# A row-wise log-softmax whose tiles take every second row of 64 instead of 32 neighbouring rows

## The chip, the core and the metric

The kernel runs on one core of a Trainium2 chip. The core has five engines with their own instruction queues: TensorE (PE) for matrix products, VectorE (DVE) for elementwise work and reductions, ScalarE (ACT) for functions such as the exponential, GpSimd (POOL) and SyncE (SP), which here only issues loads. Data move between the chip's main memory (DRAM, also called HBM) and the on-chip memory (SBUF, 128 partitions) by 16 DMA engines, which serve the transfers that SP and ACT issue. Engines are kept in step by semaphores. The metric is the time of one execution on the device in microseconds (us); less is better.

## The reference

The input is 16 x 512 x 50000 numbers of type float32, that is 8192 rows of 50000. Each row is treated by itself:

```python
max_x = np.max(x, axis=-1, keepdims=True)
shifted = x - max_x
log_sum_exp = np.log(np.sum(np.exp(shifted), axis=-1, keepdims=True))
return (shifted - log_sum_exp).astype(np.float32)
```

The input has 1638.4 MB, and so has the output. Each element is read once and written once.

## The kernel before

The 8192 rows are cut into 256 tiles of 32 rows. A row of 50000 is cut into G = 4 runs of 12500, and each run lies in a partition of its own, so that a tile fills 128 partitions x 12500 elements (6.4 MB). The partition number is 4 times the row's number in the tile plus the number of the run. Four buffers (`NBUF`) of that size take turns: tile t lies in buffer t mod 4, is worked on in place and is stored from there.

For a whole tile, VectorE takes the maximum over four columns of 3125 elements (line 221), ScalarE the exponential of each with its sum (line 276), VectorE joins the maxima of the four partitions of a row through a transposition of 32 x 32 blocks (lines 188 to 204), TensorE adds the four partial sums of a row with a matrix of ones (line 330), ScalarE takes the logarithm (line 264), and VectorE subtracts both from the tile (line 209). Since a row's four runs are always four neighbouring partitions, these steps do not depend on which rows of the input a tile holds.

Tile 0 is treated another way, so that work can start early. It is cut by rows into `NS` = 4 parts of 8 rows. A row is then cut into 16 runs of 3125, so that a part fills 128 partitions x 3125 elements. Each part has a load of its own (line 163) and a store of its own (line 268). The last tile is stored in four pieces by columns.

Order is written out by hand. SP issues the four part loads, then the loads of tiles 1 to 3, and then, for each further tile, waits until the buffer that it needs has been stored (`take(sync, stored[j])`) and issues the load (line 160). Tiles 5 and on are issued in a loop on the device, where a tile's place in DRAM is worked out from the loop's counter; the helper `run` makes the access pattern for that from the list of all tiles. ScalarE issues the store of a tile after the second of the four exponentials of the next tile (`GATE` = 2), for tiles 1 and on in a loop of the same kind. A transfer counts its semaphore up by 16 when it is complete.

In DRAM a tile of before is one piece: its 32 rows are neighbours, so its 128 runs of 12500 elements follow each other, and the access pattern has 128 runs at a step of 12500. A part of tile 0 has 128 runs of 3125 at a step of 3125. On the SBUF side there are 128 partitions in both.

Of the kernel before, what the change touches and what calls it, by code (L numbers as in the profile page):

```python
# [16 lines left out]
G = 4  # L17
R = P // G
C = 3125
NBUF = 4  # L20

NS = 4

GATE = 2
GS = G * NS
RS = P // GS
# [20 lines left out]
def take(engine, sem, n=16):  # L47

    engine.wait_ge(sem, n).then_inc(sem, -n)  # L49


def cols(c):
    return slice(c * C, (c + 1) * C)
# [3 lines left out]
def kernel(  # L57
# [6 lines left out]
    xf = x.flatten_outer_dims()  # L64
    of = out.flatten_outer_dims()
# [3 lines left out]
    ntiles = N // R  # L69


    rounds = (ntiles - NBUF) // NBUF
    assert ntiles % NBUF == 0 and rounds >= 2
    tail = range(1 + rounds * NBUF, ntiles)

    xt = xf.rearrange("(t r) (g w) -> t (r g) w", r=R, g=G)
    ot = of.rearrange("(t r) (g w) -> t (r g) w", r=R, g=G)
    xs = xf.rearrange("(t s r) (g w) -> t s (r g) w", s=NS, r=RS, g=GS)
    os = of.rearrange("(t s r) (g w) -> t s (r g) w", s=NS, r=RS, g=GS)

    def run(a, first, n):

        part = a[first : first + NBUF * n].rearrange("(q i) p w -> q i p w", i=NBUF)
        return lambda q, i: part[bass.ds(q, 1), i].rearrange("o p w -> (o p) w")

    data = ctx.enter_context(tc.tile_pool(name="data", bufs=1))
    stats = ctx.enter_context(tc.tile_pool(name="stats", bufs=1))
# [10 lines left out]
    bufs = [data.tile([P, W], FP32, name=f"buf{j}") for j in range(NBUF)]  # L98
# [41 lines left out]
    @block.gpsimd  # L140
    def _(gpsimd):
        k = 0
        for g in (GS, G):
            view = ones[g].rearrange("p (r g) -> p r g", g=g)
            r = P // g
            gpsimd.memset(ones[g], 1.0).then_inc(ready)
            gpsimd.affine_select(  # L147
                out=view, in_=view, pattern=[[-g, r], [0, g]], base=0,
                channel_multiplier=1, compare_op=ALU.is_ge, fill=0.0,
            ).wait_op(ready, k + 1, "sem-ge").then_inc(ready)  # L150
            gpsimd.affine_select(  # L151
                out=view, in_=view, pattern=[[g, r], [0, g]], base=g - 1,
                channel_multiplier=-1, compare_op=ALU.is_ge, fill=0.0,
            ).wait_op(ready, k + 2, "sem-ge").then_inc(ready)
            k += 3

    @block.sync
    def _(sync):
        def load(j, src):
            sync.dma_start(out=bufs[j], in_=src).then_inc(landed[j], 16)  # L160

        for s in range(NS):
            sync.dma_start(out=bufs[0][:, cols(s)], in_=xs[0, s]).then_inc(
                landed_part[s], 16
            )
        for t in range(1, NBUF):
            load(t, xt[t])
        take(sync, stored[0], 16 * NS)
        load(0, xt[NBUF])
        src = run(xt, NBUF + 1, rounds - 1)  # L170
        with sync.Fori(0, rounds - 1) as q:
            for i in range(NBUF):
                j = (i + 1) % NBUF
                take(sync, stored[j])
                load(j, src(q, i))
        for t in tail:
            take(sync, stored[t % NBUF])
            load(t % NBUF, xt[t])
        for j in range(NBUF - 1):
            take(sync, stored[j])  # L180
        take(sync, stored[NBUF - 1], 16 * NS)
# [78 lines left out]
    @block.scalar  # L260
    def _(scalar):
        def log(k):
            added.next(
                scalar.activation(out=logs[k], in_=rowsums[k], func=ACT.Ln)  # L264
            ).then_inc(logged.sem)

        def store(j, dst, buf):
            subtracted.next(scalar.dma_start(out=dst, in_=buf)).then_inc(stored[j], 16)

        def whole(j, dst=None):  # L270

            for c in range(NS):
                if c == GATE and dst is not None:
                    store((j - 1) % NBUF, dst, bufs[(j - 1) % NBUF])
                shifted.next(
                    scalar.activation(  # L276
                        out=dump, in_=bufs[j][:, cols(c)], func=ACT.Exp,
                        bias=negms[j][:, c : c + 1], scale=1.0,
                        accum_out=parts[j][:, c : c + 1],
                    )  # L280
                ).then_inc(on_act.sem)
                on_act.next(scalar.nop())  # L282
            agreed.next(
                scalar.activation(  # L284
                    out=scales[j], in_=negms[j], func=ACT.Exp,
                    bias=negmaxs[j][:, 0:1], scale=-1.0,
                )
            ).then_inc(rescaled.sem)
            log(j)

        def in_parts(j, t):
            for s in range(NS):
                agreed.next(
                    scalar.activation(  # L294
                        out=dump, in_=bufs[j][:, cols(s)], func=ACT.Exp,
                        bias=negmaxs[NBUF + s][:, 0:1], scale=1.0,
                        accum_out=sub_sum[:, s : s + 1],
                    )
                ).then_inc(summed_part.sem)
                if s:  # L300
                    store(j, os[t, s - 1], bufs[j][:, cols(s - 1)])
                log(NBUF + s)
            store(j, os[t, NS - 1], bufs[j][:, cols(NS - 1)])

        def settle():
            for count in (on_act, shifted, agreed, added, subtracted):
                count.settle(scalar)

        nc.scalar.preload_act_table_set("natural_log_exp_and_others")  # L309
        in_parts(0, 0)  # L310
        settle()
        whole(1)
        settle()
        dst = run(ot, 1, rounds)
        with scalar.Fori(0, rounds) as q:
            for i in range(NBUF):
                whole((i + 2) % NBUF, dst(q, i))
            settle()
        for t in tail[1:-1]:
            whole(t % NBUF, ot[t - 1])  # L320
        store(t % NBUF, ot[t], bufs[t % NBUF])
        whole(NBUF - 1)
        for c in range(NS):
            store(NBUF - 1, ot[ntiles - 1][:, cols(c)], bufs[NBUF - 1][:, cols(c)])

    @block.tensor
    def _(tensor):
# [58 lines left out]
```

## Time and profile before

| | |
|---|---|
| median of 5 runs | 7586.57 us (7585.56 to 7593.28) |
| the profiled execution: its time, and its span on the page | 7587.51 us, 7585.8 us |
| VectorE busy | 5444.0 us (72%) |
| ScalarE busy | 3184.9 us (42%) |
| TensorE busy | 478.2 us (6%) |
| bytes moved by DMA, mean rate | 3276.85 MB, 432 GB/s |
| load of a tile (255), from issue to landing | 36.7 us (median) |
| store of a tile (254), from issue to landing | 41.7 us (median) |
| load of a part of tile 0 (4) | 11.4 us (median; 6.5 to 16.3) |
| store of a part of tile 0 or a piece of the last tile (8) | 18.9 us (median) |

The span runs from the first to the last instruction; the execution's own time also has what lies around it, here 1.7 us. A busy share is an average over the span. A row of slices shows the span in 40 equal pieces, each with a digit for tenths of busy time. In a row of waits stand the instruction that waited, what released it, and then the time in total, how often, and the longest. DVEq and SPq are the queues of VectorE and SP; line 49 is the helper `take`, which waits for a transfer's semaphore. A DMA queue's row has its packets, its megabytes and its share of the time of 16 engines; q1 holds the loads and q10 the stores. A transfer is made of packets, here one for each run, and of small ones that count up the semaphore.

### The profile page before, as it was taken

The page shows a single profiled execution, that of the slowest core. Times are in us where ns is not written, and L with a number is a line of the kernel's source. Part 1 is how long each engine was busy: PE and PEld are TensorE (multiplying, and loading weights), DVE is VectorE, ACT ScalarE, POOL GpSimd, SP SyncE. Part 2 cuts the span into 40 slices and gives each one's busy share as a digit, 9 for nine tenths or more (in the row PEclk, how much of TensorE's full clock was granted, in tenths as well). Part 3 has the DMA queues.
Part 4 walks back from the last instruction along what each step waited for, and adds up shares of the span by engine and source line. Part 5 has one row for each costly group of instructions (what it writes and reads, how often), then busy time and mean ns, then how long its engine had stood idle before and what let it go on. Part 6 is the DMA issues. An engine that isn't in the chain of part 4 may idle for free. (4 is left out here: it accounts for less than half of the span.)

```text
span 7585.8 us, 13839 instructions
## 1 busy us (share of the span) xinstructions
PE 478.2 (6%) x2048; PEld 456.0 (6%) x2048; DVE 5444.0 (72%) x2832; ACT 3184.9 (42%) x2563; POOL 2.3 (0%) x10
## 2 busy tenths in 40 slices
PE   0000000000000000000000000000000000000000
PEld 0000000000000000000000000000000000000000
DVE  7777777777777777777777777777777777777776
ACT  4344443444434444344443444434444343444433
POOL 0000000000000000000000000000000000000000
DMA  9999999999999999999999999999999999999999
GB/s 423 433 433 434 433 433 433 435 434 433 435 432 434 433 433 434 433 432 435 431 434 434 431 434 433 432 433 432 435 433 432 434 432 433 433 432 434 431 434 398
DMA packets 75026, 3276.85 MB, mean 432 GB/s; under 512 B 8336, under 2 KB 8336, under 8 KB 8336
## 3 DMA queue, kind: packets, MB, share of 16 engines
q1 hardware_dynamic: 37296, 1638.42, 50.0%
q10 hardware_dynamic: 37728, 1638.42, 50.0%
q14 instruction: 2, 0.02, 0.0%
HBM read 1638.40 MB, written 1638.40 MB: 432 GB/s over the span
## 5 line engine op out<-in xcount | busy, mean ns | idle before, releaser
L276 ACT ACTIVATE dump<-buf,negm 128x3125 f32<-128x3125 f32 x1020 | 2925.7, 2868 | 3787.1 <-DVE negm L221 3748.8
L221 DVE TENSOR_REDUCE negm<-buf 128x1 f32<-128x3125 f32 x1020 | 3405.0, 3401 | 912.1 <-DVEq L49 912.1
L209 DVE TENSOR_SCALAR buf<-buf,negmax,logsum 128x12500 f32<-128x12500 f32 (+1 forms) x262 | 1739.6, 6641 | 553.5 <-ACT logsum L264 553.5
L330 PE MATMUL sums<-scaled,ones 128*128 128x1 f32 x2040 | 475.9, 355 | 7054.4 <-DVE scaled L232 7054.4
L330 PEld LDWEIGHTS sums<-scaled,ones 128*128 128x128 f32 x2040 | 454.0, 327 | 7076.3 <-DVE scaled L232 7076.3
L232 DVE TENSOR_TENSOR scaled<-scale,part 128x4 f32<-128x4 f32 x255 | 41.5, 163 | 577.7 <-ACT scale L284 577.7
L264 ACT ACTIVATE logsum<-sums 128x1 f32<-128x1 f32 x259 | 44.3, 171 | 551.5 <-PE sums L330 548.8
L276 ACT ACTIVATION_READ_ACCUMULATOR dump<-buf,negm 128x1 f32 x1020 | 190.0, 186 | 0.0
L284 ACT ACTIVATE scale<-negm,negmax 128x4 f32<-128x4 f32 x255 | 75.8, 297 | 23.5
L226 DVE TENSOR_REDUCE negp<-negm 128x1 f32<-128x4 f32 x255 | 40.1, 157 | 39.0 <-DVE negm L221 39.0
L204 DVE STREAM_TRANSPOSE negmax<-spread 128x32 f32<-128x32 f32 x259 | 54.9, 212 | 9.0
L188 DVE STREAM_TRANSPOSE allneg<-negp 128x32 f32<-128x32 f32 x259 | 54.8, 212 | 9.0
L191 DVE TENSOR_REDUCE rowneg<-allneg 128x8 f32<-128x32 f32 (+1 forms) x259 | 48.2, 186 | 9.0
L198 DVE COPY spread<-rowneg 128x32 f32<-128x32 f32 x259 | 47.0, 181 | 9.0
L239 DVE TENSOR_REDUCE negp<-buf 128x1 f32<-128x3125 f32 x4 | 13.6, 3400 | 7.6 <-DVEq L49 7.6
L294 ACT ACTIVATE dump<-buf,negmax 128x3125 f32<-128x3125 f32 x4 | 11.5, 2869 | 14.5 <-DVE negmax L204 14.5
L341 PE MATMUL sums<-sub_sum,ones 128*128 128x1 f32 x8 | 2.3, 363 | 29.6 <-ACT dump L294 29.6
L341 PEld LDWEIGHTS sums<-sub_sum,ones 128*128 128x128 f32 x8 | 2.0, 312 | 29.9 <-ACT dump L294 29.9
L309 ACT ACT_TABLE_LOAD x1 | 1.3, 1283 | 1.0 <-SPq L118 1.0
L147 POOL TENSOR_SCALAR_AFFINE_SELECT ones<-ones 128x128 f32<-128x128 f32 x2 | 0.9, 442 | 0.1
L151 POOL TENSOR_SCALAR_AFFINE_SELECT ones<-ones 128x128 f32<-128x128 f32 x2 | 0.9, 429 | 0.1
L294 ACT ACTIVATION_READ_ACCUMULATOR dump<-buf,negmax 128x1 f32 x4 | 0.7, 186 | 0.0
(5 smaller groups left out, 0.8 us busy)
## 6 DMA issues: line engine op xcount, KB each, us to landing
buf<-in_x_dram SPq DMA_DIRECT2D x255, 6250.0 KB, 36.7
out_dram<-buf ACTq DMA_DIRECT2D x254, 6250.0 KB, 41.7
out_dram<-buf ACTq DMA_DIRECT2D x8, 1562.5 KB, 18.9
buf<-in_x_dram SPq DMA_DIRECT2D x4, 1562.5 KB, 11.4
```

Of the source, the lines that this page charges most:

```text
L188: vector.transpose(out=allneg, in_=negp.to_broadcast([P, SQ]))
L191: vector.tensor_reduce(out=rowneg[:, : SQ // g], in_=allneg.rearrange("p (r g) -> p r g", g=g), op=op, axis=AX, negate=negate,)
L198: vector.tensor_copy(out=spread.rearrange("p (r g) -> p r g", g=g), in_=rowneg[:, : SQ // g, None].to_broadcast([P, SQ // g, g]),)
L204: vector.transpose(out=negmaxs[k], in_=spread)
L209: ins = vector.tensor_scalar(out=buf, in0=buf, scalar1=negmaxs[k][:, 0:1], scalar2=logs[k], op0=ALU.add, op1=ALU.subtract,)
L221: vector.tensor_reduce(out=negms[j][:, c : c + 1], in_=bufs[j][:, cols(c)], op=ALU.max, axis=AX, negate=True,).then_inc(shifted.sem if c < ...
L226: vector.tensor_reduce(out=negp, in_=negms[j], op=ALU.min, axis=AX).then_inc(on_dve.sem)
L232: vector.tensor_mul(out=scaleds[j], in0=scales[j], in1=parts[j])
L264: scalar.activation(out=logs[k], in_=rowsums[k], func=ACT.Ln)
L276: scalar.activation(out=dump, in_=bufs[j][:, cols(c)], func=ACT.Exp, bias=negms[j][:, c : c + 1], scale=1.0, accum_out=parts[j][:, c : c + 1],
L284: scalar.activation(out=scales[j], in_=negms[j], func=ACT.Exp, bias=negmaxs[j][:, 0:1], scale=-1.0,)
L330: ins = tensor.matmul(rowsums[j], ones[G], scaleds[j][:, c : c + 1], start=c == 0, stop=c == NS - 1,)
```

## The change

A tile now takes 32 rows out of 64 neighbouring ones, every second row. Tiles 0 and 1 share the first 64 rows: tile 0 has the even ones, tile 1 the odd ones; tiles 2 and 3 share the next 64, and so on. The parts of tile 0 take 8 of 16 neighbouring rows in the same way. Loads and stores use the same rows, so the output is the same.

In DRAM a tile becomes 32 rows at a step of 100000 elements (400000 bytes), each with 4 runs of 12500; the access pattern has three dimensions, 32 x 4 x 12500. A part of tile 0 becomes 8 rows at that step, each with 16 runs of 3125: 8 x 16 x 3125. The SBUF side still has 128 partitions, and which partition holds which row and run of the tile is as before. The number and size of the runs, the order of all instructions and all semaphores are as before.

The helper `combs` makes the list of tiles and the array with the half (`h`) as its first dimension; `run` now picks the half and the pair of tiles from the tile's number, and steps by k = 2 pairs from one pass of the loop to the next.

```diff
-    xt = xf.rearrange("(t r) (g w) -> t (r g) w", r=R, g=G)
-    ot = of.rearrange("(t r) (g w) -> t (r g) w", r=R, g=G)
-    xs = xf.rearrange("(t s r) (g w) -> t s (r g) w", s=NS, r=RS, g=GS)
-    os = of.rearrange("(t s r) (g w) -> t s (r g) w", s=NS, r=RS, g=GS)
-
-    def run(a, first, n):
-
-        part = a[first : first + NBUF * n].rearrange("(q i) p w -> q i p w", i=NBUF)
-        return lambda q, i: part[bass.ds(q, 1), i].rearrange("o p w -> (o p) w")
+
+    def combs(a):
+        both = a.rearrange("(t r h) (g w) -> h t r g w", h=2, r=R, g=G)
+        return [both[t % 2, t // 2] for t in range(ntiles)], both
+
+    (xt, xh), (ot, oh) = combs(xf), combs(of)
+    xs, os = (
+        a.rearrange("(t s r h) (g w) -> h t s r g w", h=2, s=NS, r=RS, g=GS)[0]
+        for a in (xf, of)
+    )
+
+    def run(both, first, n):
+
+        k = NBUF // 2
+
+        def tile_of(q, i):
+            h, t = (first + i) % 2, (first + i) // 2
+            part = both[h, t : t + k * (n - 1) + 1 : k]
+            return part[bass.ds(q, 1)].rearrange("o r g w -> (o r) g w")
+
+        return tile_of
...
-        src = run(xt, NBUF + 1, rounds - 1)
+        src = run(xh, NBUF + 1, rounds - 1)
...
-        dst = run(ot, 1, rounds)
+        dst = run(oh, 1, rounds)
...
-            store(NBUF - 1, ot[ntiles - 1][:, cols(c)], bufs[NBUF - 1][:, cols(c)])
+            store(NBUF - 1, ot[ntiles - 1][:, :, cols(c)], bufs[NBUF - 1][:, cols(c)])
```

## The prediction

> **What bounds the kernel now.** I read the page's slices first, then the DMA part, then the busiest groups, then the waits.
>
> ```profile
> span 7585.8 us, 13839 instructions
> ...
> DVE  7777777777777777777777777777777777777776
> ACT  4344443444434444344443444434444343444433
> ...
> DMA  9999999999999999999999999999999999999999
> ...
> DMA packets 75026, 3276.85 MB, mean 432 GB/s; under 512 B 8336, under 2 KB 8336, under 8 KB 8336
> ...
> q1 hardware_dynamic: 37296, 1638.42, 50.0%
> q10 hardware_dynamic: 37728, 1638.42, 50.0%
> ...
> HBM read 1638.40 MB, written 1638.40 MB: 432 GB/s over the span
> ```
>
> The DMA engines are full in all 40 slices and the two queues take half of their time each.[...] So time is bytes over the rate of 16 DMA engines: 432 / 16 = 27.0 GB/s each. One number is for later: the 8336 smallest packets are 16 x (259 loads + 262 stores). These are the completion marks: today every transfer runs on all 16 engines and leaves one mark per engine.
>
> The waits of VectorE and of the load queue say the same:
>
> ```profile
> DVE negm L221 <- DVEq L49: 912.1, 252, 4.8
> ```
>
> ```profile
> SPq L49 <- SPq L49: 7429.7, 256, 74.1
> ```
>
> VectorE idles 912.1 / 252 = 3.6 us per tile until its tile has landed, and the load queue waits 7429.7 / 256 = 29.0 us per tile for a buffer to be stored. Both wait for the DMA engines. The stretches (columns: length, busy time of PE, PEld, DVE, ACT, POOL, clock, DMA share, GB/s) show where the engines are not full:
>
> ```profile
> 0.00:75.00 75.00, 4.22 (x16) 3.79 (x16) 56.29 (x39) 33.34 (x28) 2.30 (x10) 1.00 0.97 411
> 75.00:150.00 75.00, 5.60 (x24) 5.34 (x24) 58.02 (x32) 32.66 (x27) 0.00 (x0) 1.00 1.01 429
> 3000.00:3100.00 100.00, 7.46 (x32) 7.12 (x32) 68.79 (x41) 41.12 (x36) 0.00 (x0) 1.00 1.01 435
> 7530.00:7586.00 56.00, 3.73 (x16) 3.56 (x16) 28.78 (x16) 13.10 (x14) 0.00 (x0) 1.00 0.74 315
> ```
>
> The start is full after the first 2.5 us. Only the last 56 us, with the last tile's arithmetic between its load and its store, have room. Work added to a DMA engine at the start therefore moves the end.
>
> The trace's packet records, which no printed view lists, add two things. A packet of 50,000 bytes takes 1.847 us and one of 12,500 bytes 0.467 us, nearly all of them to within 1%: an engine serves them one by one at 27 GB/s, whatever the address. And the completion marks of one engine come later and later: 2.6 us behind the first at load 8, 4.0 at load 60, 16.6 from load 120 to the last. The other fifteen need 29.52 us per tile (loads 20 to 60); 198 more tiles at that rate put their last load 20.6 us before the laggard's. So one lagging engine sets the end, and its number isn't recorded.
>
> **The change, part by part.** Arithmetic, its order, semaphores and buffers are untouched: every engine has the same instructions in the same order. All 521 transfers get another DRAM pattern; each still moves one run of 50,000 or 12,500 bytes per partition, so bytes and data packets stay.
>
> *Whole tiles (255 loads, 254 stores, and the last tile's four stores by columns).* The DRAM side goes from 128 runs in a row to 32 rows of 4 runs, one row in two left out. [...] Packets stay at 1.847 us: cost 0. [...] Our row pitch becomes 400,000 bytes, no power of two, and the flat 1.847 us says that the engine limits, not the memory. [...]
>
> *Issue.* A DMA issue takes 0.33 us on SP (L160). If a third dimension doubled it, 255 issues cost SP 84 us, inside its 7429.7 us of waiting, and ScalarE's queue 262 x 0.34 = 89 us, inside its 3748.8 us of waiting for L221. Behind such a store on ScalarE stand two exponentials, for which VectorE would wait. A load's start would be 0.33 us later, which is covered while other transfers are queued: 36.7 us to land a load and 41.7 for a store make 78.4 us in flight per tile of 29.6, 2.6 transfers at any time. Without that cover: +84. I take 0.
>
> *Tile 0 (four loads, L163, and four stores).* Here the DRAM side becomes 8 rows of 16 runs, in place of 128 runs. [...] Each of engines 0 to 7 then gets 64 loads and 64 stores of 12,500 bytes instead of 32 and 32, and engines 8 to 15 none. At today's 0.467 us that is 64 more packets x 0.467 = +29.9 us on engines that have no free time until the tail.
>
> *Which partitions these 8 engines reach.* With 128 partitions on 8 engines, the plain share is 16 neighbours each. [...] Each part then takes two shares: 0.934 us instead of 0.467. Tile 0 costs an engine 128 x 0.934 = 119.6 us against 64 x 0.467 = 29.9: +89.7. [...] Three share a port then, for some 55 us (3 tiles x 8 packets x 1.847 = 44.3, slowed by about a fifth): 55 / 1.40 = 39 packets instead of 59, 20 x 0.934 = +18.5. Sum on the slowest engines: +108. If sharing hurts loads only, or stores only, half of the 90 goes: 45 + 18.5 = +63.
>
> [...]
>
> *What is late next.* The first part lands at about 25 us (2.5 + 16 packets x 1.40) instead of 7.6, the fourth near 100 (its packets alternate with the first stores by then), tile 0 is stored some 108 us later than today, and so the load that waits for buffer 0 (the first wait on SP, 74.1 us today) starts that much later. VectorE needs 25.9 us per tile from the start of one maximum to the next (37.79 to 63.68 us), less than 29.6, so it adds nothing; nor can it catch up, since the DMA engines set the pace.
>
> *The laggard.* If it is one of 0 to 7, all of +108 reaches the end. If it is one of 8 to 15, engines 0 to 7 must first use up the 20.6 us that they are ahead: +87. I take the middle, +98. Sum against the profiled execution: 7587.5 + 98 = 7685. Its 7587.5 lies 0.9 above the median, nothing beside these costs.
>
> **Rivals.**
>
> *No port sharing.* Eight engines, each packet at 0.467 us: +30 with the laggard below 8, 7617. For it: the trace has never shown a slow port. [...]
>
> *Not slower: the laggard hides it.* Again no port sharing, and the lagging engine among 8 to 15. Engines 0 to 7 are then +29.9 - 20.6 = +9 against today's end: 7597, within 0.2%. It decides as long as tile 0's extra stays below 20.6 + 15 = 36 us; with shared ports it can't.
>
> *The split doesn't change.* The parts still run on 16 engines: 7587. [...]
>
> [...]
>
> *The lag goes.* Another address pattern frees the laggard: 20.6 us less, 7567, and nothing added.
>
> **How the numbers follow.** Shared ports 0.60, with its own range from +63 - 20.6 = +42 (7630) to +108 (7696). No sharing 0.20, half of it (laggard below 8) at 7617 and half at 7597. Split unchanged 0.07. Whole tiles slower 0.10. Lag gone 0.03. A measurement tells apart about 0.2%, 15 us. Slower: 0.60 + 0.10 + 0.10 = 0.80; same: 0.10 + 0.07 = 0.17; faster 0.03. The range reaches from 7595, below the +9 case, to 7706, leaving out the unchanged split, the freed lag and the slow tiles.
>
> **What will show it.** Smallest packets 8336 - 8 x 8 = 8272 say that eight transfers ran on 8 engines; 8336 say the split stayed. The L163 loads landing after about 25 to 100 us say shared ports; 9 to 40 say twice the packets at full speed; 6.5 to 16.3 no change. The DMA share in the first 100 us must fall, since engines 8 to 15 run dry. In the middle, 435 GB/s per stretch says that whole tiles are untouched. The prediction is wrong if the middle slows, or if paired engines fall out of step so that ports cost little.

## The result and the profile after

The changed kernel takes 7666.17 us (median of 29 executions, 7656.88 to 7699.93); the kernel before, on the same chips, 7588.06 us (median of 52). The difference of the medians is 78.1 us. The ratio of the mean times is 1.0082, 95% interval [1.0063, 1.0101]: slower by about 1%. (Some executions of most kernels here, of the one before too, take mostly 80 to 150 us longer: 10 of the 52 before took 7666 to 7683 us and pull this ratio down, which is 1.0105 without them, and the longest are left out of the ratios below.) The profiled execution took 7664.22 us with a span of 7662.5 us, 76.7 us more than before.

The rates of the 40 slices before:

```profile
GB/s 423 433 433 434 433 433 433 435 434 433 435 432 434 433 433 434 433 432 435 431 434 434 431 434 433 432 433 432 435 433 432 434 432 433 433 432 434 431 434 398
```

The slices and the DMA part of the page of the changed kernel:

```profile
span 7662.5 us, 13839 instructions
...
DVE  4677777777777777777777777777777777777776
...
DMA  8999999999999999999999999999999999999999
GB/s 243 431 433 434 432 434 434 434 432 433 434 433 432 434 432 434 432 434 432 434 433 432 434 434 433 432 434 434 431 434 434 434 432 434 433 431 434 434 434 403
DMA packets 74962, 3276.85 MB, mean 428 GB/s; under 512 B 8272, under 2 KB 8272, under 8 KB 8272
...
q1 hardware_dynamic: 37264, 1638.42, 50.1%
q10 hardware_dynamic: 37696, 1638.42, 49.6%
```

Two readings matter. The loss is in the first slice, which moved 243 GB/s where it had moved 423; from the second slice on the rate is that of before. And the small packets are 8272 = 8336 - 8 x 8: eight transfers now leave eight marks instead of sixteen, four of them loads (q1 has 32 packets fewer) and four stores (q10 likewise). These are tile 0's.

When tile 0's parts land is seen where VectorE begins their maxima (timelines: start, duration, engine, line, what). Before:

```profile
7.63 3.41 DVE L239 TENSOR_REDUCE negp<-buf 128x1 f32<-128x3125 f32 x1 [7.63 <-DVEq L49]
11.89 3.40 DVE L239 TENSOR_REDUCE negp<-buf 128x1 f32<-128x3125 f32 x1
17.92 3.40 DVE L239 TENSOR_REDUCE negp<-buf 128x1 f32<-128x3125 f32 x1
23.96 3.40 DVE L239 TENSOR_REDUCE negp<-buf 128x1 f32<-128x3125 f32 x1
```

In the changed kernel:

```profile
23.80 3.41 DVE L251 TENSOR_REDUCE negp<-buf 128x1 f32<-128x3125 f32 x1 [23.80 <-DVEq L49]
45.19 3.41 DVE L251 TENSOR_REDUCE negp<-buf 128x1 f32<-128x3125 f32 x1 [17.06 <-DVEq L49]
66.63 3.41 DVE L251 TENSOR_REDUCE negp<-buf 128x1 f32<-128x3125 f32 x1 [15.30 <-DVEq L49]
90.33 3.41 DVE L251 TENSOR_REDUCE negp<-buf 128x1 f32<-128x3125 f32 x1 [17.57 <-DVEq L49]
```

Before, only the first had a wait. Now a part lands every 21 to 24 us and VectorE stands idle for most of that. The load that waits for buffer 0 waits 153.1 us instead of 74.1 (the longest wait of the load queue):

```profile
SPq L49 <- SPq L49: 7445.7, 256, 153.1
```

Two stretches of before, then those of the changed kernel (length, busy times, clock, DMA share, GB/s at the end):

```profile
0.00:45.00 45.00, 2.35 (x8) 2.01 (x8) 31.01 (x27) 17.38 (x16) 2.30 (x10) 1.00 0.96 400
45.00:90.00 45.00, 3.74 (x16) 3.57 (x16) 35.56 (x21) 21.43 (x18) 0.00 (x0) 1.00 1.01 425
```

```profile
0.00:45.00 45.00, 0.59 (x2) 0.50 (x2) 4.20 (x5) 4.45 (x4) 2.29 (x10) 1.00 0.95 147
45.00:90.00 45.00, 1.17 (x4) 1.00 (x4) 11.98 (x12) 6.33 (x6) 0.00 (x0) 1.00 1.00 208
90.00:150.00 60.00, 2.45 (x10) 2.28 (x10) 43.36 (x27) 25.74 (x20) 0.00 (x0) 1.00 0.63 263
3000.00:3100.00 100.00, 5.60 (x24) 5.34 (x24) 71.45 (x35) 37.30 (x30) 0.00 (x0) 1.00 1.00 434
```

For 90 us all DMA engines count as busy and move a third to a half of their bytes: they aren't idle, their packets take long. Only between 90 and 150 us does the share fall, to 0.63, because eight engines have run out of work: of the sixteen marks of tile 3's load eight come at 103 us and the other eight at 145 to 146. The packet records of the trace say how long a packet takes (a table made from them; medians in its first two rows, times counted from the first transfer). They do not name a packet's engine or its partitions. Which engine serves which partitions, and that engines meet at shared ways into SBUF (the "ports" of the prediction and of the expectations), are therefore assumptions of the author's throughout; the runs show the patterns, the number of marks and the times.

| first 50 us; tile 0's packets as a whole below | before | after |
|---|---|---|
| load packet of 12,500 bytes (tile 0) | 0.468 us | 1.341 us |
| load packet of 50,000 bytes (tiles 1 to 3) | 1.847 us | 5.268 us |
| all load packets of tile 0, in engine time | 249.4 us on 16 engines | 574.7 us on 8 |
| all store packets of tile 0, in engine time | 239.7 us on 16 engines | 333.6 us on 8 |

On the average of its engines the part loads grew from 249.4 / 16 = 15.6 to 574.7 / 8 = 71.8 us (+56.2), the part stores from 15.0 to 41.7 (+26.7): together +83. At load 8 (tile 5, the four parts counted as loads 0 to 3) the last engine's completion mark is 86.9 us later than before, at the last load 76.6 us.

### The profile page after: what moved, and what is told of

Same layout as the page of the kernel before. It is cut to its first block, busy times and chain, and to the rows that moved or that the text cites. A ratio compares the mean times of both kernels' runs of the same rounds, so it can differ in the third digit from the quotient of the medians.

```text
span 7662.5 us, 13839 instructions
## 1 busy us (share of the span) xinstructions
PE 478.4 (6%) x2048; PEld 456.2 (6%) x2048; DVE 5444.4 (71%) x2832; ACT 3184.8 (42%) x2563; POOL 2.3 (0%) x10
## 2 busy tenths in 40 slices
DMA packets 74962, 3276.85 MB, mean 428 GB/s; under 512 B 8272, under 2 KB 8272, under 8 KB 8272
```

## The experiments

Theory A: the whole cost is tile 0, because its eight transfers run on 8 engines which get in each other's way ("shared ports", the assumption named above). Theory B: the whole tiles pay, by the wider row step or by the dearer issue. A weaker form of A: only the number of engines counts, twice the packets for each. The diffs show the main lines of an edit; `...` stands where others are left out.

**Which tiles pay.** First every second row for tiles 0 and 1 alone; the loads and the first stores are picked by tile:

```diff
+    xs = xf[: 2 * R].rearrange("(s r h) (g w) -> h s r g w", h=2, s=NS, g=GS)[:1]
+    xc = xf[: 2 * R].rearrange("(r h) (g w) -> h r g w", h=2, g=G)
...
-            load(t, xt[t])
+            load(t, xt[t] if t > 1 else xc[1])
...
```

> Every second row for tiles 0 and 1 alone (tile 0 in four parts, 8 rows x 16 runs); tiles 2 to 255 stay 32 neighbouring rows. Theory A (the cost is tile 0's eight transfers on 8 engines, with shared ports): the whole of the change's cost is here, +76 us, about 7664. Theory B (it is the whole tiles' wider row step or their dearer issue): no change, 7588. Mixed: in between, and the next kernel makes up the rest.

Measured: 7661.15 us (median of 4; 7659.84 to 7661.62, and once 7815.31) against 7587.74, ratio 1.0096 [1.0078, 1.0113]; +73.4 us. All but some 5 of the 78 us are here.

Then the complement, every second row for all tiles but 0 and 1:

```diff
-        return [both[t % 2, t // 2] for t in range(ntiles)], both
+        flat = a.rearrange("(t r) (g w) -> t (r g) w", r=R, g=G)
+        return [flat[t] if t < 2 else both[t % 2, t // 2] for t in range(ntiles)], both
...
```

> The complement: tiles 0 and 1 as before, every second row for tiles 2 to 255 (253 loads and stores as 32 rows x 4 runs). Theory A: 7588, within 0.2% of before, although each issue takes 0.54 us on SP instead of 0.33. Theory B: +76 us, 7664. Completion marks: all transfers on 16 engines, so 8336 small packets.

Measured: once 7587.73 us, five times 7713 to 7729. One execution at the time of before shows that the wide step doesn't have to cost anything. Whether it causes the five others was asked of the same kernel once more:

> The same kernel as the one with every second row in tiles 2 to 255 and tiles 0 and 1 as before, once more, since its times lay far apart (7587.7 once, 7713 to 7729 five times). If the wide row step costs nothing by itself, part of the runs are again at 7588 (or at 7567, where no engine lags); if it causes the slower executions, most are again 120 to 140 us longer, and more often than those of the kernel before.

Measured: median 7569.63 of 15 executions, against a median of 7585.63 for the kernel before on the same chip; ratio 0.9994 [0.9953, 1.0034]. The interval alone would allow some 26 us. But ten of the 15 lie between 7567.9 and 7572.7, and the lowest group of before, 16 of 37, between 7566.6 and 7569.2: by itself the wide row step costs some 1 us, if anything. The other five took 7656 to 7716 us, where eight of the 37 before took over 7610; that the step makes these more frequent is neither shown nor excluded. The profile of this run shows the dearer issue beside the unchanged rate (SP's issues of whole tiles: shortest, median and longest in ns; then two stretches):

```profile
L173 SPq DMA_DIRECT2D buf<-in_x_dram x255: 534/538/645, 3.4 to 7484.9; - x128
```

```profile
0.00:75.00 75.00, 4.21 (x16) 3.78 (x16) 56.01 (x39) 33.18 (x28) 2.30 (x10) 1.00 0.97 411
3000.00:3100.00 100.00, 5.60 (x24) 5.34 (x24) 71.84 (x35) 37.30 (x30) 0.00 (x0) 1.00 1.00 434
```

An issue takes 0.538 us instead of 0.333, 255 of them some 52 us more on SP, and none of it reaches the end. Theory B falls.

**Loads and stores apart.** Tile 0's loads alone, then its stores alone, with 8 rows x 16 runs; the other side keeps 128 runs in a row. Diff of the first (the second changes `os` and the stores in the same way):

```diff
-    xs = xf.rearrange("(t s r) (g w) -> t s (r g) w", s=NS, r=RS, g=GS)
+    xs = xf[: 2 * R].rearrange("(s r h) (g w) -> h s r g w", h=2, s=NS, g=GS)[:1]
...
```

> Only tile 0's four part loads have 8 rows x 16 runs (rows 0, 2, ... 62; tile 1 loads the odd ones); all stores are as before, 128 runs in a row. (Rows of tiles 0 and 1 are therefore stored in another order than they were read.) From the changed kernel's packets: 8 engines spend 574.7 / 8 = 71.8 us on part loads where 16 spent 249.4 / 16 = 15.6, so +56 us, about 7644. The count of packets alone would give +15, 7603.

> Only tile 0's four part stores have 8 rows x 16 runs; loads as before. (Rows of tiles 0 and 1 are stored in another order than they were read.) From the changed kernel's packets: (576.3 - 241.2) / 8 = 41.9 us on part stores where 16 engines spent 15.1, so +27 us, about 7615; the count of packets alone would give +15, 7603. If stores don't share a port's bandwidth the packets stay at 0.468 us.

Measured: loads 7647.96 (median of 12), +61.5 us, ratio 1.0081 [1.0052, 1.0109]; stores 7613.08 (median of 13), +26.6 us, ratio 1.0032 [1.0002, 1.0063]. Both are where the changed kernel's packets had put them, and together (88) a little more than the two at once (73 to 78). In the run with stores alone the median store packet of tile 0 stayed at 0.468 us: there the cost is above all the doubled number of packets, 64 for an engine instead of 32 (8304 marks, 32 fewer than before; +15). The mean packet took 0.60 us. The rest, some 8.5 us per engine, fell almost wholly after 68 us of the span, when whole tiles were being stored beside the parts: until then the mean was 0.48 us, from then on 0.66.

**Sharing or the number of engines.** SP holds tiles 1 to 3 back until tile 0 has landed, so that the part loads run alone:

```diff
...
+        sync.wait_ge(arrived, 1)
         for t in range(1, NBUF):
             load(t, xt[t] if t > 1 else xc[1])
...
```

> As the kernel with every second row for tiles 0 and 1 alone, but SP holds the loads of tiles 1 to 3 until tile 0's fourth part has landed, so that nothing else is under way beside the part loads. The total is longer by the hold and not compared. The packet of 12,500 bytes tells: sharing in pairs alone 0.93 us, a part every 15 us; full speed 0.467 us, every 7.5 us, if the 1.40 us of the changed kernel came from the tiles beside them; 1.40 us, every 21 us, if eight engines with this split are that slow by themselves.

Measured: the median packet of the first 30 us is 0.87 us, and a part lands every 12 to 15 us (maxima at 17.40, 30.21, 42.62 and 57.85 us). Eight engines alone (DMA share 0.50 to 0.53) move 124 GB/s, 15.5 each, instead of the 27 of an engine in the kernel before:

```profile
2.50:15.00 12.50, 0.00 (x0) 0.00 (x0) 0.00 (x0) 0.00 (x0) 0.83 (x2) 1.00 0.53 124
15.00:30.00 15.00, 0.59 (x2) 0.50 (x2) 4.20 (x5) 3.16 (x3) 0.00 (x0) 1.00 0.50 127
```

So they are slowed even without the whole tiles, by 0.87 / 0.468 = 1.86; why by less than two was not shown. Next, each part of tile 0 as 16 half rows x 8 runs (rows 0 to 15 and 16 to 31, first and second half): sixteen engines, as the 8336 marks say, but by the author's assumption with 8 neighbouring partitions each, so that two would meet at a port:

```diff
-    xs = xf.rearrange("(t s r) (g w) -> t s (r g) w", s=NS, r=RS, g=GS)
+    xh = xf[:R].rearrange("(u r) (e g w) -> u e r g w", u=2, e=2, g=GS // 2)
...
```

> [...] All else as before. (A part holds halves of rows, so tile 0's normalization is over half rows of two rows.) Shared ports: packets of 0.93 us instead of 0.467, 32 loads and 32 stores per engine, +15 + 15 = +30 us, 7618. If only the number of engines matters: 7588 and packets of 0.467 us.

Measured: load packets of 0.935 us, twice the time with all 16 engines at work, and 219 GB/s while the parts load:

```profile
2.50:15.00 12.50, 0.00 (x0) 0.00 (x0) 2.94 (x1) 0.00 (x0) 0.83 (x2) 1.00 1.00 219
15.00:30.00 15.00, 1.18 (x4) 1.01 (x4) 10.62 (x12) 6.33 (x6) 0.00 (x0) 1.00 1.02 220
```

The stores stayed at 0.468 us until the first tile was stored beside them (mean 0.77 us from 90 us on). In engine time the loads took 472.9 / 16 = 29.6 us instead of 15.6, +14, and the medians say +13.7 (7600.14 of 13 executions against 7586.43); the interval of the ratio, 1.0018 [0.9977, 1.0059], can't tell that from nothing. The packets can. So do the two groups into which the shorter times of both kernels fall: 7583 to 7584 and 7600 to 7603 here, 7567 to 7568 and 7586 to 7590 before, +16 and +14. The number of engines isn't what makes a load slow, and half of what was expected, the stores' half, didn't come.

Then each part by four transfers of 32 partitions (8 rows x 4 runs), each still on 8 engines: 8464 marks, eight for each of the 32 small transfers and sixteen for the other 513. Bytes, packets and packets per engine are those of the changed kernel; by the same assumption the eight engines of a transfer would not meet:

```diff
+            for k in range(4):
+                sync.dma_start(
+                    out=bufs[0][32 * k : 32 * k + 32, cols(s)], in_=xq[s, k]
+                ).then_inc(landed_part[s], 16)
...
```

> [...] All else as before. (In tile 0 the runs of different rows come together in one group of partitions, so its normalization is not that of its rows.) Shared ports as the cause: packets near 0.47 us while partitions 0 to 63 are served, slower only where engines 8 to 15 are at work on the same ports; total +30 to +45, 7618 to 7633. If eight engines are slow whatever ports they use: packets of 1.40 us and +76, 7664.

Measured: the median packet is 0.468 us in the first 9 us, with 8 engines at 200 GB/s (2.5 to 10 us of the span, share 0.51), 25 for each. From 14 to 32 us, once the tiles' loads have begun, it swings between 0.47 and 0.99 us. The profiled execution has 7626.31 us, +39; but four executions spread from 7625 to 7695 (median 7639.49, ratio 1.0093 [1.0064, 1.0121]), so the total alone proves little. Eight engines are not slow by their number. In this run and the one before it the rows have the same step in DRAM, 200,000 bytes, so that the row step isn't what makes packets slow. A run with the DRAM pattern of the changed kernel and other partitions was not made.

**Whole tiles as 16 x 8.** If the pattern of 16 x 8 is at fault, whole tiles must suffer from it too. Tiles 0 and 1 are as before; tiles 2 to 255 take every second pair of rows of 64, which is 16 double rows x 8 runs (by the author's assumption again 8 neighbouring partitions for an engine):

```diff
-        both = a.rearrange("(t r h) (g w) -> h t r g w", h=2, r=R, g=G)
+        both = a.rearrange("(t r h v) (g w) -> h t r (v g) w", h=2, r=R // 2, v=2, g=G)
...
```

> [...] Bytes, packets and the 50,000 bytes per packet are as before. Shared ports: in every tile two engines meet at a port; if they stay in step the transfer takes twice as long, up to 15,000 us, and if they fall out of step (one at its first group of four partitions, the other at its second) little is lost, 7600 to 8000. If ports don't matter: 7588.

Measured: 9993.29 us (median of 4), ratio 1.3199 [1.3057, 1.3341]. All 16 engines work (8336 marks), with the bytes and packets of before, and the middle runs at 344 GB/s instead of 435:

```profile
3000.00:3100.00 100.00, 5.60 (x24) 5.34 (x24) 52.82 (x26) 26.04 (x24) 0.00 (x0) 1.00 1.00 344
```

Between 1000 and 9000 us a load packet takes 2.97 us (median), a store packet 1.98, against 1.847 for both. The loads, which write into SBUF, suffer (+61%), the stores, which read out of it, hardly (+7%), though they have the same pattern in DRAM.

**Who is held up.** One thing of the first 50 us was not explained: the packets of tiles 1 to 3 were as slow as those of the parts (50,000 / 5.268 and 12,500 / 1.341 are 9.5 and 9.3 GB/s). Here the parts are loaded by halves, partitions 0 to 63 first. By the author's assumption engines 0 to 7 then meet in pairs, while the other eight load tile 1 into partitions 64 to 127, where no other engine is at work:

```diff
...
+        half(0)
+        load(1, xt[1])
+        half(1)
...
```

> Each part of tile 0 is loaded by two transfers of 64 partitions (8 rows x 8 runs), on 8 engines with 8 neighbouring partitions each. SP issues the four for partitions 0 to 63, then tile 1, then the four for partitions 64 to 127, then tiles 2 and 3. (Tile 0's partitions hold half rows of two rows and are stored as before, so its output is not that of its rows.) [...] If an engine is slowed only by engines at its own port: packets of tile 1 take 1.85 us there and parts 0.93 us. If two engines at one port hold up others too, as the 5.3 us packets of engines 8 to 15 in the changed kernel suggest: tile 1's first packets take 3.5 to 5.3 us.

Measured, with times counted from the first transfer: in the first 28 us the parts' packets take 0.94 us and tile 1's packets 3.53 us (59 of them, median). Between 45 and 78 us, when by the same assumption parts and tiles go to the same partitions, it is 1.38 and 5.19 us. In the stretches (of the span):

```profile
2.50:15.00 12.50, 0.00 (x0) 0.00 (x0) 0.00 (x0) 0.00 (x0) 0.82 (x2) 1.00 0.93 210
15.00:30.00 15.00, 0.00 (x0) 0.00 (x0) 0.00 (x0) 0.00 (x0) 0.00 (x0) 1.00 0.99 220
45.00:75.00 30.00, 0.59 (x2) 0.50 (x2) 9.80 (x11) 4.54 (x4) 0.00 (x0) 1.00 0.99 154
```

12,500 / 0.94 and 50,000 / 3.53 are 13.3 and 14.2 GB/s: half of the full 27 for both kinds of packets alike. Later it is a third for both, 9.0 and 9.6. So the packets of a whole tile are slow while part loads of this pattern are under way; that tile 1's first ones go to other partitions is the assumption, and how they are held up wasn't tried.

**Two attempts at a better kernel.** Every second row everywhere, but with tile 0 in four pieces by columns, 32 rows x 4 runs, so that no transfer has 8 as its slowest dimension (8288 marks, 16 for each of its 518 transfers):

```diff
-            sync.dma_start(out=bufs[0][:, cols(s)], in_=xs[0, s]).then_inc(
+            sync.dma_start(out=bufs[0][:, cols(s)], in_=xt[0][:, :, cols(s)]).then_inc(
...
```

> Every second row everywhere, but tile 0 comes in four pieces by columns (32 rows x 4 runs of 3125) in place of four parts by rows, and is then treated and stored as a whole tile. [...] Theory A (engines and ports of tile 0 alone made the cost): 7588, within 20 us, packets of 0.467 us at the start. If the wide row step or the dearer issue costs anything: 7600 or more.

Measured: at the start the expected packets of 0.468 us, parts landing from 7.70 to 18.93 us and no loss. But 15 executions lie between 7598 and 7817 us (median 7711.46, ratio 1.0088 [1.0042, 1.0133]). Its profile, of an execution of 7719.32 us, shows full speed up to the seventh slice and then less:

```profile
GB/s 416 433 433 432 434 433 432 427 423 424 427 422 423 423 423 423 423 427 426 424 423 423 423 423 427 423 423 423 427 423 427 425 423 425 427 423 423 424 426 395
```

So the start is mended and the time isn't. In the later slices it is stores that take longer: a twentieth of their packets of 50,000 bytes took over 2.5 us, against 1.847 in the median. Why is open; the next kernel's profile shows the same without a wide row step.

The last attempt has nothing to do with the change: the kernel before, with its last tile loaded by columns, so that most of its 13.4 us of maxima lie ahead of the last landing.

```diff
+        for c in range(NS):
+            sync.dma_start(
+                out=bufs[NBUF - 1][:, cols(c)], in_=xt[ntiles - 1][:, cols(c)]
+            ).then_inc(landed_part[c], 16)
...
```

> The kernel before with one change at its end: the last tile is loaded in four pieces by columns, so that three of its four maxima (3.4 us each) and exponentials run before the last piece has landed. From the end of before, where 13.4 us of maxima stand between the last landing and the rest: 10 us less, 7577; nothing if the pieces land together, since each engine serves its packets in order and the lagging one is 16 us late.

Measured: median 7644.28 us of 14 executions (four at 7579.7 to 7580.7, the rest up to 7705), ratio 1.0032 [0.9985, 1.0079]. The kernel before had executions at 7567 on that chip; there is no gain to show.

## Why the prediction was right, and where its steps were wrong

**Bound and path.** Right. Time is what the busiest DMA engines have to do, and a delay in the first 100 us went to the end: +86.9 us in the last completion mark at load 8, +76.6 at the last load. The first part landed at 23.8 us (put at about 25), the fourth at 90 (near 100), and the wait for buffer 0 grew by 79 us (some 108).

**Whole tiles and issue at 0.** Right, shown by the repeated complement (0.9994) and by 434 GB/s in the middle. Slower whole tiles, given a chance of 0.10, didn't come at the step of 400,000 bytes. The issue became dearer by 0.21 us (0.538 instead of 0.333), within the 0.33 that was allowed for, and stayed covered.

**Tile 0 on 8 engines.** Right: 8272 completion marks, as written. That the eight are engines 0 to 7, with 16 neighbouring partitions each, was the author's assumption, which no run shows.

**Shared ports.** No run shows the ports. The 0.934 us of the sum, twice the measured 0.467 for loads and stores alike, was the author's assumption; what the runs showed in its place is a doubling of load packets in some patterns: 0.935 us for 16 half rows x 8 runs on 16 engines, 0.468 us for 8 rows x 4 runs on 8, and +32% in time for whole tiles as 16 x 8. Part loads were put at 44.9 + 18.5 = +63 us for an engine and took +56.2. The mis-sized term is the stores: +44.9 by the same doubling, +26.7 measured. The step "each part takes two shares: 0.934 us instead of 0.467" fails for stores. The doubling was taken for both directions, where the runs show it for loads: the changed kernel's part stores, 8 rows x 16 runs on 8 engines, ran at full speed, 0.468 us, from 92 to 138 us of the span. They were slow while part loads ran beside them (0.80 us, until 92 us) and again beside the stores of whole tiles (mean 0.73 us, from 138 us on). Of the +26.7 us some 15 are the doubled packets and 6 each of these two.

**The third share.** No run shows three engines at one port: the 1.40 us and the +18.5 of the sum were assumed with it. The step had the packets of whole tiles slowed by about a fifth, and the DMA share falling in the first 100 us because the engines without parts run dry. Wrong: those packets took 2.85 times as long (5.268 us instead of 1.847) and the share stayed at 0.95 to 1.00 until 90 us. In the run by halves, too, packets of parts and of whole tiles were slowed alike (13.3 and 14.2 GB/s). It cost little in the sum, because the engines without parts don't set the end: they are through with tile 3 at 103 us, 42 us before the others. Part packets of 1.34 us, close to the 1.40 of the sum, are therefore right in size for a reason that is in part wrong and for the rest not shown.

**The laggard.** Put at 0 to -21, taken as -10; the marks give 76.6 - 86.9 = -10.3 between load 8 and the last load. That the middle of two cases was met is luck, since it is neither of the two: four engines bring up the rear in the changed kernel, by some 16 us from load 8 to the end, and the one of before isn't to be found among them by number. That 20.6 us is what the laggard costs is supported by the kernel before on two other chips, where many executions take 7567 us in place of 7587, and by the trace of the repeated complement (7567.97 us): at tile 253 its last engine is 6 us behind the first, in the kernel before 17.

**The sum.** +83 (56.2 + 26.7) on the engines and -10 from the laggard make +73, against +108 and -10. Of the 25 us between them the stores are 18 and the loads 7. The measured +78 lies some 5 above that sum, for which no run gives a cause. The prediction's other case, sharing by loads alone, is the one that the runs come near, but its sum is wrong: halving the 90 also halves what the doubled packets of the stores cost at full speed. By its own terms, of which no run shows the third share, it is 44.8 for the loads, 15 for the stores and 18.5 for the third share, +78 for the engines and not +63.

**Rivals.** No sharing (7617 or 7597), an unchanged split (7587) and slower whole tiles are all out. Their one trace is the pattern of pairs of rows, where the whole tiles became slower (9993.29 us).

## What to carry to other kernels

Here a transfer's pattern decided how many DMA engines it used (16 marks for 32 x 4 and 16 x 8, 8 marks for 8 x 16 and 8 x 4) and how long its load packets took, even when bytes, runs and packets stayed the same. Where DMA sets the time, look at the slowest dimension first: 32 x 4 ran on 16 engines and was free, 8 x 16 ran on 8 and cost 78 us in a single tile, and 16 x 8 ran on 16 engines and cost 32% in nearly all tiles. So sixteen engines are not enough; that each of them needs partitions apart from the others' would fit these times and was not shown. The small packets on the page counted the engines (8336 = 16 x 521 before, 8272 with eight transfers on 8), and packet time against size (1.341 us for 12,500 bytes instead of 0.468) told slow packets from idle engines.

## What the runs showed of the hardware

- Beside part loads of 8 rows x 8 runs, whose packets took 0.94 us instead of 0.468, packets of a whole tile's load took 3.53 us instead of 1.847, and later 5.19 us beside 1.38. Both kinds then moved at about one rate for an engine, 13 to 14 and 9 to 10 GB/s.
- Stores weren't slowed in this way: 0.468 us per packet (median) as 8 rows x 16 runs on 8 engines and as 16 half rows x 8 runs on 16, where loads of the second pattern took 0.935. They took longer only beside part loads (0.80 us) or beside stores of whole tiles (means of 0.66 to 0.77 us).
- A busy share of DMA near 1.00 said nothing of the rate: 208 GB/s (45 to 90 us) and 434 GB/s (in the middle) were both 1.00.
- With a third dimension in the pattern the median issue of a whole tile took 0.538 us instead of 0.333 on SP, and of a store 0.554 instead of 0.338 on ScalarE.
